# Query-state products of a retention layer as plain float32 products in 32-column strips

## The chip, the cores and the metric

The kernel runs on one core of a Trainium2 chip. The metric is the device time of one execution in microseconds. A core has five engines that run their own instruction queues: TensorE (PE, with its weight loads shown as PEld), VectorE (DVE), ScalarE (ACT), GpSimd (POOL) and SyncE (SP), which here only issues transfers.

## The reference

One inference step of a trunk of two layers, all in float32. Each layer normalizes its input, projects it to eight streams of 2048 channels, and runs a pooling branch and a retention branch that are gated, merged, projected and added to the input. There are 272 prompt tokens (16 of them learned) and 8 samples of 8 tokens each, 336 tokens in all. The part that the change touches is the retention of the samples, with a given state S of 256 x 256 for each of the 8 heads:

```python
def retention_chunk(S, q, k, v):
    ...
    scores = jnp.einsum('bihd,bjhd->bhij', q, k) * decay[None]
    intra = jnp.einsum('bhij,bjhe->bihe', scores, v)
    q_decay = jnp.exp((idx[:, None] + 1.0) * lg[None, :])
    inter = jnp.einsum('bihd,bhde->bihe', q, S) * q_decay[None, :, :, None]
    k_decay = jnp.exp((n - 1.0 - idx)[:, None] * lg[None, :])
    S_new = S * jnp.exp(n * lg)[None, :, None, None] + jnp.einsum('bjhd,bjhe->bhde', k * k_decay[None, :, :, None], v)
    return S_new, intra + inter
```

`inter` is the query-state product: 8 tokens of a sample times its own state, 8 x 256 by 256 x 256, for 8 samples, 8 heads and 2 layers.

## The kernel before

Tokens lie along the free dimension, channels along the partitions, so a projection is a product whose moving operand is the activations (128 x 336 or 128 x 320) and whose stationary operand is a block of weights. To keep float32 precision at the speed of the faster type float32r, every operand x is split into hi, x rounded to float32r (`hi_of`, line 158, on ScalarE), and lo = x - hi (`lo_of`, line 164, on VectorE), and a product is made of three: hi hi, hi lo, lo hi.

The program is one list of steps. In each step the main loop (from line 853) issues the load of a weight tile four steps ahead on SyncE's queue (`dma_step`, line 177), its split two steps ahead, then the 24 products of this step (`main_step`; every product is issued at line 154), and then the events that were put down for the step with `at`. An event's instructions go to the queues of their engines behind those of the step's products. Every head of a layer takes 16 steps (four for each of k, v, q and the gate), and its events run on into the next head's steps; `E(d, fn)` puts an event at step d of the head.

For the samples of a head it does the following. `sload(b)` loads a state (256 KB) into one of five buffers named sraw, on SyncE's queue, for samples 0 to 4 at steps 8 to 12 and for samples 5 to 7 at steps 17 to 19. `split_q` at step 12 splits q and lets GpSimd copy the sample columns of hi and lo into qpad, a tile that holds, for each half of the channels and each sample, 128 stationary columns, all zero but the sample's own 8 columns of hi and 8 of lo. `ssplit(b)` splits a state into shi and slo. `sdo(b)` at step 15 + b multiplies the 128 columns of qpad with shi and slo, both halves of the channels, into one bank of PSUM, where the products of all samples add up (each writes zeros to the rows of the others); then it makes the state's update from kts and vbd (`up`), adds it to the decayed state in place (line 423, VectorE) and stores it from GpSimd's queue (line 424). `inter_copy` at step 23 scales the bank and splits it into ithi and itlo, and `pv(2)` at step 24 adds it to the samples' outputs with two products with the matrix c01, which also sums the rows of hi and lo.

PSUM has four banks for all this (tag side). A stationary operand with few columns whose output begins at partition 0 sits in the first 32-column strip of TensorE's array; in the kernel before these are the products with 16 output rows in `pv(2)` (line 472).

`spread_rstd` (line 229) and the warm-up of 12 products before the first step are plain float32 products, and `tok` (line 313) and `back` (line 490) transpose float32 tiles.

Of the kernel before, what the change touches and what calls it, by code (L numbers as in the profile page):

```python
# [6 lines left out]
F32 = mybir.dt.float32  # L7
F32R = mybir.dt.float32r
# [6 lines left out]
NM = 16  # L15
SEQ = 256
NP = NM + SEQ
NB = 8
NS = 8
T = NP + NB * NS  # L20
HEADS = 8
HD = 256
# [15 lines left out]
C_C01 = C_GQ + 8  # L38
# [4 lines left out]
def tables():  # L43
    import numpy as np

    f = np.float32
    lg = np.log1p(-np.exp2(f(-5.0) - np.arange(HEADS, dtype=f))).astype(f).astype(np.float64)
    pos = np.concatenate([np.arange(NP), 2048 + np.tile(np.arange(NS), NB)]).astype(f)
    inv = (10000.0 ** (-np.arange(128) / 128)).astype(f)
    ang = (pos[None, :] * inv[:, None]).astype(f).astype(np.float64)  # L50
    cst = np.zeros((128, C_W), f)
    cst[:, C_ID:C_ID + 128] = np.eye(128)
    cst[:, C_COS:C_COS + T] = np.cos(ang)
    cst[:, C_SIN:C_SIN + T] = np.sin(ang)
    r = np.arange(128)
    for h in range(HEADS):
        for b in range(2):
            cst[:, C_KD + 3 * h + b] = np.exp((NP - 1 - b * 128 - r) * lg[h]) / 16
        cst[:NR2, C_KD + 3 * h + 2] = np.exp(np.where(r < NM, NM - 1 - r, NS - 1 - (r - NM) % NS) * lg[h])[:NR2] / 16
        cst[:, C_GQ + h] = np.exp((r % 8 + 1) * lg[h])  # L60
    cst[r, C_C01 + NM + r % 64] = 1
    for g, w in enumerate(WINDOWS):
        cst[:, C_RC + 16 * g:C_RC + 16 * g + 16] = 1.0 / np.minimum(w, np.arange(16) + 1)
    dt = np.zeros((HEADS, 128, SC), f)
    tok = np.arange(T)
    prompt = tok < NP
    for h in range(HEADS):
        jj, ii = tok[:, None], tok[None, :]
        same = np.where(prompt[:, None], prompt[None, :], (~prompt[None, :]) & ((jj - NP) // NS == (ii - NP) // NS))
        m = np.where(same & (ii >= jj), np.exp(np.maximum(ii - jj, 0) * lg[h]) / 16, 0)  # L70
        dt[h, :, 0:NR0] = m[0:128, 0:NP]
        dt[h, :, NR0:NR0 + NR1] = m[128:256, 128:NP]
        dt[h, :NR2, NR0 + NR1:SC] = m[256:T, 256:T]
    return {"cst": cst, "dtab": dt}, [float(np.exp(NS * x)) for x in lg]


def build(tc, a, o, g8):
    nc = tc.nc
# [6 lines left out]
    def at(s, fn, *args):  # L85
        events[s].append(lambda: fn(*args))
# [15 lines left out]
    def open_pool(name, side=None, **kw):  # L102
        P[name] = tc.alloc_tile_pool(name=name, bufs=1, side=side, reuse_waits="tile", **kw)
        return P[name]
# [15 lines left out]
    def side():  # L120
        return sidep.tile([128, 512], F32, tag="side", bufs=4, name="side")
# [4 lines left out]
    cst = cp.tile([128, C_W], F32, name="cst")  # L126
# [26 lines left out]
    def mm(out, lhsT, rhs, start, stop):  # L153
        nc.tensor.matmul(out, lhsT, rhs, start=start, stop=stop)  # L154

    def hi_of(out, in_, scale=None):
        if scale is None:
            nc.scalar.copy(out=out, in_=in_)  # L158
        else:
            nc.scalar.activation(out=out, in_=in_, func=ACTF.Copy, scale=scale)  # L160

    def lo_of(out, in_, hi, scale=None):
        if scale is None:
            nc.vector.tensor_tensor(out=out, in0=in_, in1=hi.bitcast(F32), op=ALU.subtract)  # L164
        else:
            nc.vector.scalar_tensor_tensor(out=out, in0=in_, scalar=scale, in1=hi.bitcast(F32),  # L166
                                           op0=ALU.mult, op1=ALU.subtract)
# [78 lines left out]
    H = {}  # L246

    for l in range(DEPTH):
# [12 lines left out]

        def open_r(l=l, a_side=a_side):
            p = open_pool("r", side=a_side)
            t = p.tile([128, 2, 8, 128], F32R, name="qpad")
            nc.gpsimd.memset(t.bitcast(F32), 0.0)
            H["qpad"] = t
            t = p.tile([128, SC], F32, name="sc")
            nc.gpsimd.memset(t[64:128, NR0 + NR1:SC], 0.0)
            H["sc"] = t
            t = p.tile([128, 2, 4, HD], F32R, name="vbd")  # L270
            nc.gpsimd.memset(t.bitcast(F32), 0.0)
            H["vbd"] = t
            for key in ("kt", "vt"):
                t = p.tile([128, HD], F32R, name=key + "tail")
                nc.gpsimd.memset(t[64:128].bitcast(F32), 0.0)
                H[key + "tail"] = t
# [4 lines left out]
        def head(h, l=l, c0=c0, n=n, nt=nt):  # L281
            hs = {}
            rp = lambda shape, dt, tag, bufs=1: P["r"].tile(shape, dt, tag=tag, bufs=bufs, name=tag)
# [73 lines left out]
            def split_q():  # L357
                qr = hs["qr"]
                qhi, qlo = rp([128, 2, T], F32R, "qhi"), rp([128, 2, T], F32R, "qlo")
                hi_of(qhi[:, :, n], qr[:, :, n])  # L360
                lo_of(qlo[:, :, n], qr[:, :, n], qhi[:, :, n])
                hs["q"] = qhi, qlo
                for i, s in enumerate((qhi, qlo)):
                    for d in range(2):
                        src = s[:, d, NP:T].rearrange("p (b t) -> p b t", b=8)
                        base = H["qpad"][:, d, 0, 64 * i:64 * i + 8]
                        dst = bass.AP(tensor=base.tensor, offset=base.offset, ap=[base.ap[0], [136, 8], [1, 8]])
                        nc.gpsimd.tensor_copy(out=dst, in_=src)

            def scores():  # L370
                dtab = rp([128, SC], F32, "dtab")
# [23 lines left out]
                hs["p"] = phi, plo  # L395

            def sload(b):
                s = rp([128, 2, HD], F32, "sraw", 5)
                nc.sync.dma_start(out=s, in_=a["state_ret"][l, b, h].rearrange("p (d e) -> p d e", d=2))
                hs["s", b] = s  # L400

            def ssplit(b):
                s = hs["s", b]
                hi, lo = rp([128, 2, HD], F32R, "shi", 2), rp([128, 2, HD], F32R, "slo", 2)
                hi_of(hi, s)
                lo_of(lo, s, hi)
                hs["sh", b] = hi, lo

            def sdo(b):
                if b == 0:  # L410
                    hs["inter"] = side()
                ps = hs["inter"]
                for i, x in enumerate(hs.pop(("sh", b))):
                    for d in range(2):
                        mm(ps[:, :HD], H["qpad"][:, d, b], x[:, d], b == 0 and i == 0 and d == 0,
                           b == NB - 1 and i == 1 and d == 1)
                up = side()
                for d in range(2):
                    mm(up[:, HD * d:HD * d + HD], hs["kts"][:, b // 4, 128 * d:128 * d + 128],
                       H["vbd"][:, b // 4, b % 4], True, True)  # L420
                s = hs.pop(("s", b))
                s2 = s.rearrange("p d e -> p (d e)")
                nc.vector.scalar_tensor_tensor(out=s2, in0=s2, scalar=g8[h], in1=up, op0=ALU.mult, op1=ALU.add)  # L423
                nc.gpsimd.dma_start(out=o["ret_s"][l, b, h].rearrange("p (d e) -> p d e", d=2), in_=s)  # L424
# [76 lines left out]
            E = lambda d, fn, *ar: at(b0 + d, lambda: fn(*ar))  # L501
# [10 lines left out]
            E(10 + kl, stack_out, "vt")  # L512
            E(12 + kl, stack_in, "vt")
            E(12, split_q)
            E(16, pstate)
            E(11, scores)
            E(14, scores2)
            for b in range(5):
                E(8 + b, sload, b)
            E(13, ssplit, 0)  # L520
            for b in range(NB):
                E(15 + b, sdo, b)
                if b + 1 < NB:
                    E(15 + b, ssplit, b + 1)
                if b + 5 < NB:
                    E(17 + b, sload, b + 5)
            E(17, pv, 0)
            E(18, norm2, 0)
            E(19, pv, 1)
            E(20, norm2, 1)  # L530
            E(23, inter_copy)
            E(24, pv, 2)
            E(25, norm2, 2)
            E(26, back)
# [3 lines left out]
        if l == 0:  # L538
            at(6, open_r)
        else:  # L540
            at(r0 - 1, open_r)
        for h in range(HEADS):
            head(h)
# [402 lines left out]
```

## Time and profile before

| | |
|---|---|
| median of 3 runs | 2878.2 us (2875.74 to 2878.21) |
| the profiled execution | 2874.4 us, its span 2872.7 us |
| TensorE busy | 2850.5 us (99%), 19,228 products |
| VectorE busy | 1594.3 us (55%) |
| ScalarE busy | 1001.4 us (35%) |
| GpSimd busy | 363.1 us (13%) |
| moved by DMA | 516.65 MB, 180 GB/s on average |

The rows below name an instruction by its line in the kernel, engine and operation, then the tiles (output, then inputs, where the first input named is the moving operand and the second the stationary one), the shape, and counts and times. "128*16 128x256" is a product with 128 rows and 16 columns of stationary operand and a moving operand of 256 columns. TensorE works in a pipeline, so a product lasts longer than the distance to the next one's start. "<-" behind a time of idleness names what ended it.

### The profile page before, as it was taken

What the parts mean: (1) busy time and instruction counts of PE and PEld (TensorE: products, weight loads), DVE (VectorE), ACT (ScalarE), POOL (GpSimd) and SP (SyncE); (2) the same over time, 40 slices, a digit from 0 to 9 for tenths busy, and PEclk for the clock granted to TensorE, in tenths of its full rate; (3) what the DMA queues carried; (4) which work ended last, traced back from release to release, by engine and by line L of the source; (5) the groups of instructions that cost most, each with busy time, mean ns of one, the idle gap of its engine ahead of it and who ended that gap; (6) DMA issues with size and microseconds to landing.
All of it is one profiled execution on the core that took longest, in us unless ns stands there. A gap on an engine that the chain in (4) does not pass through costs nothing.

```text
span 2872.7 us, 46777 instructions
## 1 busy us (share of the span) xinstructions
PE 2850.5 (99%) x19228; PEld 2844.3 (99%) x19228; DVE 1594.3 (55%) x2026; ACT 1001.4 (35%) x1245; POOL 363.1 (13%) x560
## 2 busy tenths in 40 slices
PE   9999999999999999999999999999999999999997
PEld 8999999999999999999999999999999999999997
DVE  7666666654345664344456666666544456644543
ACT  4333333333233333333333333333332333333332
POOL 5222222210000000000122222222100000000000
PEclk9999999999999999999999999999999999999999
DMA  6555555655454444444555665566555544444443
GB/s 225 195 200 207 204 206 203 209 199 176 160 163 155 143 151 149 143 155 166 197 179 200 209 208 208 208 207 206 204 180 180 173 145 161 144 160 162 170 161 126
DMA packets 174262, 516.65 MB, mean 180 GB/s; under 512 B 23888, under 2 KB 46672, under 8 KB 174032
## 3 DMA queue, kind: packets, MB, share of 16 engines
q1 hardware_dynamic: 150976, 447.81, 45.7%
q0 software_dynamic: 21696, 63.99, 6.2%
q8 instruction: 150, 2.46, 0.3%
q10 hardware_dynamic: 1376, 1.87, 0.2%
q14 instruction: 64, 0.52, 0.1%
HBM read 447.91 MB, written 66.57 MB: 179 GB/s over the span
## 4 chain that ended last, share of the span: by engine, by line
PE 98%; issue 1%; POOL 1%; DVE 0%; DMA 0%; ACT 0%; POOLq 0%; SPq 0%; DVEq 0%; ACTq 0%
PE acc L154 90%; PE side L154 7%; PE side L313 1%; PE side L490 0%; POOL xsq L214 0%; POOL xsq L213 0%; DMA x<-in_xT_dram 0%; DVE xf L889 0%; DVE h_lo L166 0%; DVE sinr L235 0%; POOL trs L221 0%; DVE wlo L164 0%; ACT sq L207 0%; POOLq L934 0%; DVE xs L789 0%
## 5 line engine op out<-in xcount | busy, mean ns | idle before, releaser
L154 PE MATMUL acc<-act_hi,whi 128*128 128x320 f32 (+1 forms) x3328 | 1039.7, 312 | 0.0
L154 PE MATMUL acc<-act_lo,whi 128*128 128x320 f32 (+1 forms) x3328 | 1037.5, 312 | 0.0
L154 PE MATMUL acc<-act_hi,wlo 128*128 128x320 f32 (+1 forms) x3328 | 1036.1, 311 | 0.0
L164 DVE TENSOR_TENSOR wlo<-raw,whi 128x1024 fp32r<-128x1024 f32 x720 | 870.7, 1228 | 286.5 <-ACT whi L158 277.3
L158 ACT CAST whi<-raw 128x1024 fp32r<-128x1024 f32 x720 | 738.5, 1047 | 444.7 <-PE acc L154 360.0
L154 PE MATMUL acc<-h_hi,whi 128*128 128x336 f32 x2304 | 736.6, 320 | 0.7 <-ACT whi L158 0.7
L154 PE MATMUL acc<-h_lo,whi 128*128 128x336 f32 x2304 | 733.2, 318 | 3.8 <-DVE h_lo L166 3.7
L154 PE MATMUL acc<-h_hi,wlo 128*128 128x336 f32 x2304 | 730.9, 317 | 0.7 <-DVE wlo L164 0.7
L154 PEld LDWEIGHTS acc<-act_lo,whi 128*128 128x128 f32 x3328 | 626.4, 188 | 0.0
L154 PEld LDWEIGHTS acc<-act_hi,wlo 128*128 128x128 f32 x3328 | 625.1, 188 | 0.0
L154 PEld LDWEIGHTS acc<-act_hi,whi 128*128 128x128 f32 x3328 | 624.8, 188 | 0.0
L154 PEld LDWEIGHTS acc<-h_lo,whi 128*128 128x128 f32 x2304 | 436.9, 190 | 5.3 <-DVE h_lo L166 5.2
L154 PEld LDWEIGHTS acc<-h_hi,wlo 128*128 128x128 f32 x2304 | 434.5, 189 | 1.0 <-DVE wlo L164 1.0
L154 PEld LDWEIGHTS acc<-h_hi,whi 128*128 128x128 f32 x2304 | 434.0, 188 | 0.9 <-ACT whi L158 0.9
L423 DVE SCALAR_TENSOR_TENSOR sraw<-sraw,side 128x512 f32<-128x512 f32 x128 | 87.8, 686 | 154.1 <-PE side L154 154.1
L424 POOL DMA_DIRECT2D out_ret_s_dram<-sraw x128 | 71.4, 558 | 548.2 <-DVE sraw L423 541.1
L158 ACT CAST shi<-sraw 128x512 fp32r<-128x512 f32 x128 | 79.0, 617 | 109.0 <-PE side L154 109.0
L164 DVE TENSOR_TENSOR slo<-sraw,shi 128x512 fp32r<-128x512 f32 x128 | 88.1, 688 | 0.1
L211 POOL TENSOR_TENSOR xsq<-sq 128x336 f32<-128x336 f32 (+1 forms) x3 | 3.0, 985 | 564.8 <-ACT sq L207 564.8
L160 ACT ACTIVATE kthi<-side,cst 128x256 fp32r<-128x256 f32 (+1 forms) x48 | 20.9, 468 | 137.5 <-PE side L313 137.5
L158 ACT CAST vthi<-side 128x256 fp32r<-128x256 f32 (+1 forms) x48 | 16.2, 371 | 146.3 <-PE side L313 146.3
L678 POOL DMA_DIRECT2D out_pool_u_dram<-uc x16 | 8.7, 545 | 440.5 <-DVE uc L633 440.5
(157 smaller groups left out, 2023.0 us busy)
## 6 DMA issues: line engine op xcount, KB each, us to landing
raw<-in_w_in_dram SPq DMA_DIRECT2D x512, 512.0 KB, 4.5
sraw<-in_state_ret_dram SPq DMA_DIRECT2D x128, 256.0 KB, 3.1
out_ret_s_dram<-sraw POOLq DMA_DIRECT2D x128, 256.0 KB, 3.3
raw<-in_proj_ret_dram SPq DMA_DIRECT2D x64, 512.0 KB, 4.2
raw<-in_proj_pool_dram SPq DMA_DIRECT2D x64, 512.0 KB, 5.1
raw<-in_w_out_dram SPq DMA_DIRECT2D x64, 512.0 KB, 5.2
raw<-in_pool_w_dram SPq DMA_DIRECT2D x16, 512.0 KB, 3.4
kts<-ktd SPq DMA_DIRECT2D x16, 256.0 KB, 2.9
```

Source lines behind the costliest of these rows:

```text
L154: nc.tensor.matmul(out, lhsT, rhs, start=start, stop=stop)
L158: nc.scalar.copy(out=out, in_=in_)
L160: nc.scalar.activation(out=out, in_=in_, func=ACTF.Copy, scale=scale)
L164: nc.vector.tensor_tensor(out=out, in0=in_, in1=hi.bitcast(F32), op=ALU.subtract)
L211: eng.tensor_tensor(out=xsq[:, n], in0=sq[:, 0, n], in1=sq[:, 1, n], op=ALU.add)
L313: nc.tensor.transpose(ps[:rows, 128 * d:128 * d + 128], hs[src][:, d, 128 * b:128 * b + rows], ident)
L423: nc.vector.scalar_tensor_tensor(out=s2, in0=s2, scalar=g8[h], in1=up, op0=ALU.mult, op1=ALU.add)
L424: nc.gpsimd.dma_start(out=o["ret_s"][l, b, h].rearrange("p (d e) -> p d e", d=2), in_=s)
L678: nc.gpsimd.dma_start(out=o["pool_u"][l, 2 * g + i], in_=gs.pop(("uc", i)))
```

## The change

The states are no longer split. qpad becomes a float32 tile with 32 stationary columns for each half of the channels and each sample; samples 0 to 3 use columns 0 to 7 and samples 4 to 7 columns 8 to 15, the rest stays zero. GpSimd copies the sample columns into it from q as it is before the split. A new event `inter` at step 15, ahead of the first sdo, makes all query-state products of the head: 16 plain float32 products, 2 for each sample; the outputs of samples j and j + 4 go to the rows 32 j to 32 j + 31 of the bank, which is the strip j of the array, and the loops are written so that four products in a row go to four strips. All eight states have to be on chip then, so sraw has eight buffers, and the loads stand at steps 6 to 13. `inter_copy` moves from step 23 to step 16. The matrix c01 changes with the layout of the bank. The state's update and its store stay as they were.

```diff
-    cst[r, C_C01 + NM + r % 64] = 1
+    place = r[r % 32 < 16]
+    cst[place, C_C01 + NM + 8 * (place // 32) + 32 * (place % 32 // 8) + place % 8] = 1
...
-            t = p.tile([128, 2, 8, 128], F32R, name="qpad")
-            nc.gpsimd.memset(t.bitcast(F32), 0.0)
+            t = p.tile([128, 2, 8, 32], F32, name="qpad")
+            nc.gpsimd.memset(t, 0.0)
...
-                for i, s in enumerate((qhi, qlo)):
+                for half_ in range(2):
                     for d in range(2):
-                        src = s[:, d, NP:T].rearrange("p (b t) -> p b t", b=8)
-                        base = H["qpad"][:, d, 0, 64 * i:64 * i + 8]
-                        dst = bass.AP(tensor=base.tensor, offset=base.offset, ap=[base.ap[0], [136, 8], [1, 8]])
-                        nc.gpsimd.tensor_copy(out=dst, in_=src)
+                        b0_ = NP + 32 * half_
+                        nc.gpsimd.tensor_copy(out=H["qpad"][:, d, 4 * half_:4 * half_ + 4, 8 * half_:8 * half_ + 8],
+                                              in_=qr[:, d, b0_:b0_ + 32].rearrange("p (b t) -> p b t", b=4))
...
-                s = rp([128, 2, HD], F32, "sraw", 5)
+                s = rp([128, 2, HD], F32, "sraw", 8)
...
-            def ssplit(b):
-                s = hs["s", b]
-                hi, lo = rp([128, 2, HD], F32R, "shi", 2), rp([128, 2, HD], F32R, "slo", 2)
-                hi_of(hi, s)
-                lo_of(lo, s, hi)
-                hs["sh", b] = hi, lo
+            def inter():
+                ps = hs["inter"] = side()
+                for i in range(2):
+                    for d in range(2):
+                        for j in range(4):
+                            b = 4 * i + j
+                            mm(ps[32 * j:32 * j + 32, :HD], H["qpad"][:, d, b], hs["s", b][:, d],
+                               i == 0 and d == 0, i == 1 and d == 1)
 
             def sdo(b):
-                if b == 0:
-                    hs["inter"] = side()
-                ps = hs["inter"]
-                for i, x in enumerate(hs.pop(("sh", b))):
-                    for d in range(2):
-                        mm(ps[:, :HD], H["qpad"][:, d, b], x[:, d], b == 0 and i == 0 and d == 0,
-                           b == NB - 1 and i == 1 and d == 1)
                 up = side()
...
-            for b in range(5):
-                E(8 + b, sload, b)
-            E(13, ssplit, 0)
+            for b in range(NB):
+                E(6 + b, sload, b)
+            E(15, inter)
             for b in range(NB):
                 E(15 + b, sdo, b)
-                if b + 1 < NB:
-                    E(15 + b, ssplit, b + 1)
-                if b + 5 < NB:
-                    E(17 + b, sload, b + 5)
+            E(16, inter_copy)
...
-            E(23, inter_copy)
```

## Rows read from the trace of the kernel before

**Rows 1.** The page: busy time, share and instructions; granted clock by slices; chain by engine.

```profile
PE 2850.5 (99%) x19228; PEld 2844.3 (99%) x19228; DVE 1594.3 (55%) x2026; ACT 1001.4 (35%) x1245; POOL 363.1 (13%) x560
PEclk9999999999999999999999999999999999999999
...
PE 98%; issue 1%; POOL 1%; DVE 0%; DMA 0%; ACT 0%; POOLq 0%; SPq 0%; DVEq 0%; ACTq 0%
```

**Rows 2.** Groups by shape, TensorE: count | busy us, mean ns | idle before, its ender.

```profile
L154 PE MATMUL acc<-h_hi,whi 128*128 128x336 f32 x2304 | 736.6, 320 | 0.7 <-ACT whi L158 0.7
L154 PE MATMUL acc<-h_lo,whi 128*128 128x336 f32 x2304 | 733.2, 318 | 3.8 <-DVE h_lo L166 3.7
L154 PE MATMUL acc<-h_hi,wlo 128*128 128x336 f32 x2304 | 730.9, 317 | 0.7 <-DVE wlo L164 0.7
...
L154 PE MATMUL side<-shi,qpad 128*128 128x256 f32 x256 | 51.3, 282 | 0.0
L154 PE MATMUL side<-vbd,kts 128*128 128x256 f32 x256 | 51.1, 281 | 0.0
L154 PE MATMUL side<-slo,qpad 128*128 128x256 f32 x256 | 51.0, 281 | 0.0
```

**Rows 3.** Timeline of TensorE around one sdo: start us, us, instruction.

```profile
181.56 0.31 PE L154 MATMUL acc<-h_hi,wlo 128*128 128x336 f32 x1
181.72 0.41 PE L154 MATMUL side<-shi,qpad 128*128 128x256 f32 x2
181.96 0.40 PE L154 MATMUL side<-slo,qpad 128*128 128x256 f32 x2
182.19 0.40 PE L154 MATMUL side<-vbd,kts 128*128 128x256 f32 x2
182.43 0.32 PE L154 MATMUL acc<-h_hi,whi 128*128 128x336 f32 x1
182.59 0.32 PE L154 MATMUL acc<-h_lo,whi 128*128 128x336 f32 x1
```

**Rows 4.** By tile, plain float32 products: count, ns min/median/max, first and last start, shapes.

```profile
L154 PE MATMUL side<-ones x24: 275/421/579, 1.1 to 5.7; 128*128 128x128 f32 x24
...
L154 PE MATMUL side<-cst,sinr x12: 271/275/582, 42.1 to 2859.9; 128*128 128x128 f32 x12
```

**Rows 5.** Timeline of TensorE at spread_rstd; busy time, clock by windows there.

```profile
42.62 0.35 PE L154 MATMUL side<-cst,cosr 80*128 80x80 f32 x2
42.76 0.40 PE L154 MATMUL acc<-h_hi,whi 128*128 128x336 f32 x1
...
core 0: us, PE busy (x) PEld busy (x) DVE busy (x) ACT busy (x) POOL busy (x), PEclk, DMA share, GB/s
42.00:43.00 1.00, 0.93 (x8) 0.94 (x9) 0.08 (x2) 0.00 (x1) 0.94 (x2) 1.00 0.83 322
```

**Rows 6.** Timeline and group of the float32 transposes.

```profile
186.87 0.60 PE L313 MATMUL side<-cst,tmp 128*80 128x128 f32 x4
191.02 0.38 PE L313 MATMUL side<-cst,tmp 128*128 128x128 f32 x2
...
L313 PE MATMUL side<-cst,tmp 128*128 128x128 f32 x128 | 24.4, 272 | 0.0
```

**Rows 7.** Timeline of TensorE in pv(2), where the 16-row products stand.

```profile
195.19 0.28 PE L154 MATMUL side<-vthi,plo 80*80 80x256 f32 x1
195.31 0.28 PE L154 MATMUL side<-vthi,phi 128*16 128x256 f32 x1
195.43 0.28 PE L154 MATMUL side<-vtlo,phi 128*16 128x256 f32 x1
...
195.89 0.28 PE L154 MATMUL side<-vthi,plo 128*16 128x256 f32 x1
196.00 0.28 PE L154 MATMUL side<-ithi,c 128*80 128x256 f32 x1
```

**Rows 8.** Groups by shape, weight loads.

```profile
L154 PEld LDWEIGHTS side<-shi,qpad 128*128 128x128 f32 x256 | 42.9, 188 | 0.0
...
L154 PEld LDWEIGHTS side<-vthi,plo 128*16 128x16 f32 x32 | 3.0, 94 | 0.7
```

**Rows 9.** Groups by shape, the other engines.

```profile
L164 DVE TENSOR_TENSOR slo<-sraw,shi 128x512 fp32r<-128x512 f32 x128 | 88.1, 688 | 0.1
...
L158 ACT CAST shi<-sraw 128x512 fp32r<-128x512 f32 x128 | 79.0, 617 | 109.0 <-PE side L154 109.0
...
L368 POOL CAST qpad<-qlo 128x64 fp32r<-128x64 f32 x32 | 29.2, 938 | 0.0
...
L368 POOL CAST qpad<-qhi 128x64 fp32r<-128x64 f32 x32 | 18.0, 588 | 61.8 <-ACT qhi L158 61.8
```

**Rows 10.** Waits of SyncE's queue (total us, times, longest); sraw's transfers to landing.

```profile
SPq L177 <- DVE wlo L164: 1573.7, 510, 10.3
SPq L399 <- DMA out_ret_s_dram<-sraw: 338.0, 47, 15.1
...
DMA to landing us min/median/max: 2.2/3.2/8.0
```

## The prediction

> **What bounds the kernel now.** I read the page first. TensorE is busy for 99% of the span at a granted clock of nine tenths or more in every slice, and the chain of work that ended last is 98% TensorE; VectorE is at 55% and ScalarE at 35% [rows 1]. Next come the groups of instructions by shape: before the 6,912 projection products of 336 columns TensorE idled 5.2 us in all, and before the products with the sample states, 256 of each kind, not at all [rows 2]. So in the retention stage TensorE never waits. What shortens a TensorE instruction there shortens the kernel by as much, and what is taken from any other engine gives nothing as long as that holds.
>
> A TensorE instruction must be priced by the distance from its start to the next start, not by its length: in one loop step the projection products start every 0.15 to 0.16 us although each lasts 0.32 us, since they are pipelined [rows 3]. In that step the sample work is six instructions: two products with the upper half of the state (shi), two with the lower (slo), two for the update (vbd). From the first shi to the first vbd it is 182.19 - 181.72 = 0.47 us, so a float32r product of 256 columns costs 0.118 us.
>
> **What is removed on TensorE.** Per sample the four products with shi and slo. There are 2 layers x 8 heads x 8 samples = 128 samples, which agrees with the 256 + 256 products counted [rows 2]. 128 x 0.47 = 60.2 us, all of it on the path. Per head that is 3.76 us.
>
> **What is added on TensorE.** Per head 8 samples x 2 halves = 16 plain float32 products of 256 columns. First, how many instructions is one? The kernel before has a few plain float32 products that are no transposes: spread_rstd makes two of 128 columns in each of three calls, 6 in the source, and the trace has 12 matmuls for them; the 12 warm-up products are 24 matmuls [rows 4]. So each becomes two instructions, one right behind the other, and a head gets 32. Second, what does one instruction take? Two such instructions of 80 columns take 42.76 - 42.62 = 0.14 us at a granted clock of 1.00, or 0.07 us for 80 columns, which makes 0.224 for 256 [rows 5]. The transposes, float32 too and one instruction each, give a finer figure: four of 128 columns last 0.60 us from first start to last end, the last of them 0.272, so (0.60 - 0.272) / 3 = 0.109 us for 128 columns and 0.218 for 256 [rows 6]. That is nearly twice the 0.118 of float32r. I take 0.218. The upper bound is 0.224; the lower one is 0.216, from a pair of transposes: 0.38 us less the last one's 0.272 is 0.108 [rows 6].
>
> Narrow weights do not shorten a product. The last block of each head has products with 16 output rows, and they start 0.11 to 0.12 us apart like those of 128 rows [rows 7]. So a strip of 32 columns gains only if several strips stream at once, and no row of before shows two strips at once. This is the unknown of the change, and its bounds are far apart. If nothing overlaps, a head costs 32 x 0.218 = 6.98 us. If all four strips run independently, each carries 4 products, 8 instructions, and the head costs 8 x 0.218 = 1.74 us.
>
> Between them lies what I take. The two instructions of one product go to the same strip and stand next to each other in the queue: strip 0 twice, then strip 1 twice, and so on. The trace shows matmuls starting in program order throughout, each only when the one ahead of it has streamed its columns [rows 3, 7]. If the queue keeps that order, the second instruction of strip 0 has to wait for the first, and strip 1 stands behind it. When strip 0's second starts, strip 1's first can start with it, but strip 1's second must wait again. So two instructions overlap, not four: 32 of them take 17 slots, 17 x 0.218 = 3.71 us. I choose this as it needs no reordering, which no row shows.
>
> Strips need their weights loaded too. A load of 16 columns lasts 94 ns, one of 128 columns 188 ns [rows 8], and these overlap the running products; 32 columns lie between, so I take nothing for them. The switch between full width and a strip has a row: the 16-row products already sit in the first 32-column strip, and from the last 80-row product (195.19) to the first of them (195.31), and back (195.89 to 196.00), the distance is 0.12 and 0.11 us, the same as without a switch [rows 7]. I take zero. The Trainium skill says otherwise (TensorEngine Tiling (Array Packing), Key Properties): going to another tiling mode drains the engine. Two drains per head at the 0.28 - 0.12 = 0.16 us by which a product outlasts its slot would be 16 x 2 x 0.16 = 5.1 us; the row speaks against it.
>
> **What lies off the path.** The splitting of 128 states goes: 79.0 us of ScalarE and 88.1 us of VectorE [rows 9]. TensorE waits for neither, so nothing is gained. GpSimd's 64 copies into qpad stay 64, with half the elements; at 588 and 938 ns before [rows 9] they are done three steps ahead of the new products. The memset of qpad shrinks, off the path. The copy of the products out of PSUM moves from step 23 to 16: it keeps a side bank for one step and not for eight, which takes pressure away.
>
> The eight state loads go from steps 8 to 12 and 17 to 19 to steps 6 to 13, on SyncE's queue between the weight loads, and each must find its buffer free: with eight buffers the loads of one head wait for the stores of the same samples of the head before. Behind such a wait stand the weight loads. In the trace SyncE waits 1573.7 us for buffers of the weights and 338.0 us for state stores, with no TensorE idle [rows 10]; the queue is far ahead. A state's store is issued at steps 15 to 22 of a head, its reuse stands at 22 to 29, so the new waits are shorter than the old (there a store at 15 was followed by the load at 17). I take nothing. Were the cover gone, a late state would stop TensorE for at most its landing time, 2.2 to 8.0 us [rows 10].
>
> **The sum.** Against the profiled run (2872.7 us of span, 2874.4 in all): 2874.4 - 60.2 + 16 x 3.71 = 2873.6 us, a gain of 0.8. With 0.216 or 0.224 it is 2873.0 or 2875.1. That run lies 3.8 us under the median of 2878.2 and 1.3 under the lowest of the runs, so on the median the sum says 2877.4. I give 2876, with an own range of 2870 to 2882.
>
> **Rivals.** Four strips at once: the two instructions of a strip queue in the strip and the other strips do not wait. 2874.4 - 60.2 + 16 x 1.74 = 2842.0, or 2846 on the median. For it: nothing in TensorE's work forbids it, the strips share no output. Against it: the program order of the starts. The Trainium skill (TensorE: Matmul & The Clock Gate, Part 3) measures such packs at one product's length plus about 4 ns per further tile, which would give this result; the same section calls matmuls strictly first-in first-out, which with two instructions per strip gives mine. No run here has shown either.
>
> No strips at once, the rival on the other side: float32 streams of different strips exclude each other, and 32 instructions take 6.98 us per head: 2874.4 - 60.2 + 111.7 = 2925.9, or 2930 on the median. For it: every product in the trace streams alone [rows 3, 7]. It decides as soon as fewer than 6.98 / 3.76 = 1.86 instructions overlap on average. Against it: the strips use separate columns and separate output rows.
>
> The new products wait for the eighth state: they need all eight at step 15, where the first sample needed one. Its load stands at step 13, and SyncE runs steps ahead [rows 10]. If each head lost the median landing of 3.2 us it would be 51 us more, near 2928.
>
> **How the numbers follow.** Pairs 0.42; four at once 0.36; none at once 0.17; waiting for states 0.02; something else 0.03, split between a faster and a slower end. This kernel's measurement tells 0.2%, 5.8 us, from no change. Faster is 0.36 + 0.01 = 0.37, same 0.42, slower 0.17 + 0.02 + 0.02 = 0.21. The range reaches down to four at once with the low price (2841.8, less a little) and up to the end of the pairs' own range: 2840 to 2882; what is slower by serial strips or late states stays outside with 0.2.
>
> **What would show it.** In the timeline of a head's step 15, the stretch from the first strip product to the next full-width instruction: 3.7 us by my forecast, 1.7 with four at once, 7.0 with none. The starts inside it: pairs at one moment every 0.218 us, or single starts, or four and more together. TensorE's idle before these products near zero, and the projection products at the same distance as before. ScalarE and VectorE lighter by 79 and 88 us. The prediction fails if the queue lets strips pass each other, or if float32 keeps them apart.

## The result and the profile after

| | before | after |
|---|---|---|
| median | 2877.3 us (2875.7 to 2878.2, 4 runs) | 2846.9 us (2846.2 to 2847.1, 4 runs) |
| ratio | | 0.9896, 95% interval 0.9882 to 0.9911 |
| the profiled execution, its span | 2874.4 us, 2872.7 us | 2847.1 us, 2845.3 us |

The kernel became faster by 30.5 us on the medians and by 27.4 us between the two profiled executions. That is the time of the rival "four strips at once" (2846), not that of the forecast (2876).

From the page after: busy time and share by engine, the granted clock by slices, and the chain that ended last by engine.

```profile
PE 2821.2 (99%) x19228; PEld 2796.1 (98%) x19228; DVE 1518.4 (53%) x1898; ACT 932.8 (33%) x1117; POOL 362.4 (13%) x560
PEclk9999999999999999999999999999999999999998
...
PE 98%; issue 0%; DVE 0%; POOL 0%; POOLq 0%; ACT 0%; DVEq 0%; ACTq 0%
```

TensorE bounds the kernel as in [rows 1], with the same number of matmuls, since 512 float32r ones became 512 halves of float32 products. What changed is how they lie in time. The timeline of TensorE at step 15 of a head (start us, us, instruction), against [rows 3]:

```profile
222.53 0.31 PE L155 MATMUL acc<-h_hi,wlo 128*128 128x336 f32 x1
222.77 1.93 PE L155 MATMUL side<-sraw,qpad 128*32 128x256 f32 x32
224.63 0.50 PE L155 MATMUL side<-vbd,kts 128*128 128x256 f32 x2
224.98 0.32 PE L155 MATMUL acc<-h_hi,whi 128*128 128x336 f32 x1
```

From the first strip product to the update it is 224.63 - 222.77 = 1.86 us for the whole head. How the 32 matmuls lie in it shows when the same stretch is cut into slices of one slot. Columns: slice, its length, busy time of TensorE's matmuls with the number that run in it, the same for weight loads and GpSimd, then clock and DMA.

```profile
222.76:223.00 0.24, 0.23 (x4) 0.16 (x8) 0.00 (x0) 1.00 0.00 0
223.00:223.22 0.22, 0.22 (x8) 0.13 (x4) 0.00 (x0) 1.00 0.00 0
223.22:223.43 0.21, 0.21 (x8) 0.13 (x4) 0.00 (x0) 1.00 0.00 0
...
224.30:224.51 0.21, 0.21 (x8) 0.00 (x0) 0.00 (x0) 1.00 0.85 332
```

Four start in the first slice. In each later one there are eight: the four of the slice before, which still drain, and four new ones. So four matmuls stream at once, in eight rounds: the first lasts 0.24 us, the others 0.216. That the four are of four different strips, and not two halves of two products, is settled by the kernels with fewer strips below.

### The profile page after: what moved, and what is told of

Same layout as the page of the kernel before. It is cut to its first block, busy times and chain, and to the rows that moved or that the text cites. A ratio compares the mean times of both kernels' runs of the same rounds, so it can differ in the third digit from the quotient of the medians.

```text
span 2845.3 us, 46391 instructions
## 1 busy us (share of the span) xinstructions
PE 2821.2 (99%) x19228; PEld 2796.1 (98%) x19228; DVE 1518.4 (53%) x1898; ACT 932.8 (33%) x1117; POOL 362.4 (13%) x560
## 4 chain that ended last, share of the span: by engine, by line
PE 98%; issue 0%; DVE 0%; POOL 0%; POOLq 0%; ACT 0%; DVEq 0%; ACTq 0%
PE acc L155 91%; PE side L155 6%; PE side L314 1%; PE side L485 0%; DVE xf L880 0%; DVE h_lo L167 0%; POOLq L925 0%; POOL xsq L215 0%; POOL xsq L214 0%; DVE xs L780 0%; ACT sq L208 0%; DVEq L925 0%; DVE sinr L236 0%; POOLq L214 0%; ACTq L208 0%
## 5 line engine op out<-in xcount | busy, mean ns | idle before, releaser
L582 DVE SCALAR_TENSOR_TENSOR mb<-tr,acc 128x336 f32<-128x336 f32 (+1 forms) x32 | 14.4, 493 | 81.0 <-PE acc L155 81.0
L389 DVE TENSOR_TENSOR sc<-side,dtab 128x416 f32<-128x416 f32 (+1 forms) x16 | 9.3, 583 | 90.3 <-PE side L155 90.3
```

The costliest lines, as they stand in the source:

```text
L389: nc.vector.tensor_tensor(out=sc[:, w], in0=ps[:, w], in1=dtab[:, w], op=ALU.mult)
L582: nc.vector.scalar_tensor_tensor(out=t[:, d, n], in0=H["tr", l, i][:, d, n], scalar=1.0, in1=acc[:, d, n], op0=ALU.add, op1=ALU.mult)
```

## Experiments

All experiments start from the changed kernel; its 2846.9 us and 1.86 us per head are what they are compared with. A difference per head counts 16 times. Kernels with one execution are marked so.

### Order: strip after strip

```diff
-                for i in range(2):
-                    for d in range(2):
-                        for j in range(4):
+                for j in range(4):
+                    for i in range(2):
+                        for d in range(2):
```

> The same 16 float32 strip products per head, but ordered strip by strip: the eight instructions of strip 0, then those of strip 1, and so on. Theory A (each strip has its own line; an instruction that waits for its strip doesn't hold up those of other strips behind it, as deep as needed): starts still come four by four every 0.216 us, the stretch from the first strip product to the update stays near 1.87 us per head, the time near 2847. Theory B (program order is kept, and the four at once of the changed kernel come from looking past one or two instructions only): only neighbours of different strips overlap, the stretch is 6 to 6.9 us, the time 2847 + 16 x 4.1 to 5.0 = 2913 to 2928.

Measured: 2889.9 us. In the timeline the stretch is 231.79 - 227.27 = 4.52 us:

```profile
227.27 4.59 PE L155 MATMUL side<-sraw,qpad 128*32 128x256 f32 x32
231.79 0.50 PE L155 MATMUL side<-vbd,kts 128*128 128x256 f32 x2
```

Neither A nor B as they were put. The slices of this stretch, columns as above:

```profile
227.26:227.50 0.24, 0.23 (x1) 0.14 (x2) 0.00 (x0) 1.00 0.09 34
227.50:227.72 0.22, 0.22 (x2) 0.11 (x1) 0.00 (x0) 1.00 0.05 19
227.72:227.94 0.22, 0.22 (x2) 0.11 (x1) 0.00 (x0) 1.00 0.00 0
227.94:228.16 0.21, 0.21 (x2) 0.11 (x1) 0.00 (x0) 1.00 0.00 0
228.16:228.37 0.21, 0.21 (x3) 0.14 (x3) 0.00 (x0) 1.00 0.77 152
228.37:228.58 0.21, 0.21 (x4) 0.14 (x2) 0.00 (x0) 1.00 0.98 215
```

One matmul at a time streams for four slots: strip 0 alone. Strip 1 joins in the fifth, when three of strip 0's eight matmuls are left waiting. So a waiting matmul does let those of another strip pass, but only three may wait. Counted out, 4 slots of strip 0 alone, then 4 + 4 + 4 that two strips share, and 4 of strip 3 alone make 20 slots, 20 x 0.216 = 4.32 us; the longer first slot of each strip (0.24) and the end add 0.2. The time agrees: 16 x (4.52 - 1.86) = 42.6, hence 2889.5.

### Order: the two halves of a sample in a row

```diff
                 for i in range(2):
-                    for d in range(2):
-                        for j in range(4):
+                    for j in range(4):
+                        for d in range(2):
```

> The strip products ordered by sample, both channel halves of a sample one behind the other, so that four instructions in a row go to one strip. From the strip-after-strip run: there strip 1's first product started with strip 0's fifth, that is, once three of strip 0 were left waiting. Theory A1 (every strip can hold three waiting matmuls of its own): four in a row fit, one running and three waiting, so all four strips still stream together; first strip product to the update 1.87 to 1.92 us, the time 2847 to 2848. Theory A2 (three waiting matmuls in all, over all strips): the stretch grows to about 2.5 us, the time 2847 + 16 x 0.6 = 2857.

Measured: 2848.3 us (2847.2 to 2849.2), and the stretch is 225.20 - 223.30 = 1.90 us:

```profile
223.30 1.97 PE L155 MATMUL side<-sraw,qpad 128*32 128x256 f32 x32
225.20 0.51 PE L155 MATMUL side<-vbd,kts 128*128 128x256 f32 x2
```

The first two slices of this stretch, columns as above:

```profile
223.29:223.53 0.24, 0.23 (x4) 0.18 (x8) 0.00 (x0) 1.00 0.00 0
223.53:223.75 0.22, 0.22 (x8) 0.15 (x4) 0.00 (x0) 1.00 0.00 0
```

A1 holds: with nine matmuls of other strips waiting in the queue ahead of it, strip 3's first one still starts in the first slot. The three places belong to each strip.

### Fewer strips

Two strips with four samples each (the copies into qpad and the matrix c01 follow the new layout):

```diff
...
-                for i in range(2):
+                for i in range(4):
                     for d in range(2):
-                        for j in range(4):
-                            b = 4 * i + j
+                        for j in range(2):
+                            b = 2 * i + j
...
-                               i == 0 and d == 0, i == 1 and d == 1)
+                               i == 0 and d == 0, i == 3 and d == 1)
...
-                    mm(ps[:NR2, :HD], c01, hs["it"][0], False, False)
+                    mm(ps[:NR2, :HD], c01[:64], hs["it"][0], False, False)
```

> The samples sit in two strips, four samples in each, instead of in four. Theory A (overlap of strips is what pays): each strip carries 16 instructions, 16 x 0.216 = 3.46 us per head instead of 1.73, the time 2847 + 16 x 1.73 = 2875. Rival (a 32-column float32 product is cheap in itself because its weights are narrow, or the two instructions of a product overlap): no change, 2847.

One strip, with the same loops as the changed kernel:

```diff
-                            mm(ps[32 * j:32 * j + 32, :HD], H["qpad"][:, d, b], hs["s", b][:, d],
-                               i == 0 and d == 0, i == 1 and d == 1)
+                            mm(ps[0:32, :HD], H["qpad"][:, d, b], hs["s", b][:, d],
+                               i == 0 and d == 0 and j == 0, i == 1 and d == 1 and j == 3)
...
-                    mm(ps[:NR2, :HD], c01, hs["it"][0], False, False)
+                    mm(ps[:NR2, :HD], c01[:32], hs["it"][0], False, False)
```

> All 16 products go to the first strip (the eight samples' rows are added up, so the samples' outputs are left wrong). Theory A: 32 instructions one after another, 32 x 0.216 = 6.9 us per head, the time 2847 + 16 x 5.2 = 2930. The rival that narrow weights are cheap in themselves: 2847. The gap of 0.24 us before the first strip product and of 0.31 us behind the last ones, if they belong to the change to 32 columns: still there; if they belong to the strips beside the first: gone, as at the 16-row products of before.

Measured, one execution each: 2880.0 us with two strips, 2935.8 us with one. Timelines of the two-strip kernel and then of the one-strip kernel:

```profile
226.41 0.31 PE L155 MATMUL acc<-h_hi,wlo 128*128 128x336 f32 x1
226.65 3.65 PE L155 MATMUL side<-sraw,qpad 128*32 128x256 f32 x32
230.23 0.50 PE L155 MATMUL side<-vbd,kts 128*128 128x256 f32 x2
```

```profile
233.74 0.31 PE L155 MATMUL acc<-h_hi,wlo 128*128 128x336 f32 x1
233.97 7.09 PE L155 MATMUL side<-sraw,qpad 128*32 128x256 f32 x32
241.00 0.50 PE L155 MATMUL side<-vbd,kts 128*128 128x256 f32 x2
241.34 0.32 PE L155 MATMUL acc<-h_hi,whi 128*128 128x336 f32 x1
```

The stretches are 3.58 and 7.03 us: with 4, 2 and 1 strips 1.86, 3.58, 7.03. Theory A holds; narrow weights are worth nothing in themselves, and the two matmuls of a product do not overlap, or one strip would not take 32 slots. The stretches explain 27.5 and 82.7 us, and 33.1 and 88.9 were measured. The rest, some 6 us, I had made myself without expecting it: where fewer strips are used, the product with c01 has 64 or 32 rows and not 128, and in the two-strip kernel this stands there:

```profile
343.10 0.28 PE L155 MATMUL side<-vthi,plo 128*16 128x256 f32 x1
343.31 0.34 PE L155 MATMUL side<-ithi,c 64*80 64x256 f32 x1
343.49 0.28 PE L155 MATMUL side<-itlo,c 64*80 64x256 f32 x1
343.70 0.42 PE L155 MATMUL acc<-h_hi,whi 128*128 128x336 f32 x1
343.96 0.32 PE L155 MATMUL acc<-h_lo,whi 128*128 128x336 f32 x1
```

The distances are 0.21, 0.18, 0.21 and 0.26 us, where products with 128 rows in [rows 7] keep 0.11 to 0.12 and one projection product follows another at 0.154. From the last plo product to the second projection product it is 0.86 us, 0.36 more than the 0.50 of the changed kernel (335.44 to 335.94 in its trace), and 16 x 0.36 = 5.8 us. With 32 rows, in the one-strip kernel, the same distance is 358.15 - 357.30 = 0.85 us.

### What a change to strips costs

Full width, so no strips at all:

```diff
-            t = p.tile([128, 2, 8, 32], F32, name="qpad")
+            t = p.tile([128, 2, 8, 128], F32, name="qpad")
...
-                            mm(ps[32 * j:32 * j + 32, :HD], H["qpad"][:, d, b], hs["s", b][:, d],
+                            mm(ps[:, :HD], H["qpad"][:, d, b], hs["s", b][:, d],
```

> The 16 plain float32 products with 128 stationary columns (zeros beside the sample's own), so without strips; the samples' rows are added up as in the one-strip kernel and the outputs left wrong. Both theories: 32 instructions of 0.216 us, 6.9 us per head. It tells what the gaps at the two ends belong to: if to strips, the distance from the last projection product to the first of these is 0.154 and the one behind the last 0.216, the time some 16 x 0.2 = 3 us under the one-strip kernel; if to float32, the gaps of 0.24 and 0.31 stay.

Measured, one execution: 2923.8 us. Its timeline:

```profile
231.84 0.31 PE L155 MATMUL acc<-h_hi,wlo 128*128 128x336 f32 x1
231.99 7.07 PE L155 MATMUL side<-sraw,qpad 128*128 128x256 f32 x32
238.71 0.58 PE L155 MATMUL side<-vbd,kts 128*128 128x256 f32 x2
239.13 0.32 PE L155 MATMUL acc<-h_hi,whi 128*128 128x336 f32 x1
```

The first float32 product follows at 0.15 us, as one projection product follows another; in the strip kernels at 0.24. From that last projection product to the next one, less its own slot of 0.154 and two updates of 0.118, it is 239.13 - 231.84 - 0.39 = 6.90 us, 32 x 0.216 and nothing more. In the one-strip kernel the same sum gives 241.34 - 233.74 - 0.39 = 7.21. So the change to a strip and back costs 0.31 us, and it belongs to the strip, the first one too, not to float32. The time is 12.0 us under the one-strip kernel, where some 3 had been expected: 16 x 0.31 = 5.0 us are this price, and 5.8 are the product with c01, which keeps its 128 rows here.

Two visits to the strips per head instead of one; inter(i) makes the products of four samples:

```diff
...
-            E(15, inter)
+            E(15, inter, 0)
+            E(16, inter, 1)
...
-            E(16, inter_copy)
+            E(17, inter_copy)
```

> Samples 0 to 3 at step 15, samples 4 to 7 at step 16, so the array changes to strips and back twice per head instead of once. If each change has the price read from the one-strip and full-width kernels (0.32 us for there and back, of it 0.09 before, 0.09 behind, the rest a weight load that nothing hides), the time is 2847 + 16 x 0.32 = 2852. Rival (the gaps are a wait for the states or for qpad, or a cost of the first products only): 2847.

Measured: 2853.1 us (2851.4 to 2853.6), 6.2 more than the changed kernel where 5.1 were expected. The first visit of a head in the timeline:

```profile
153.20 0.31 PE L155 MATMUL acc<-h_hi,wlo 128*128 128x336 f32 x1
153.44 1.07 PE L155 MATMUL side<-sraw,qpad 128*32 128x256 f32 x16
154.44 0.50 PE L155 MATMUL side<-vbd,kts 128*128 128x256 f32 x2
154.78 0.31 PE L155 MATMUL acc<-h_hi,whi 128*128 128x336 f32 x1
```

It is 154.78 - 153.20 - 0.39 = 1.19 us for four rounds of 0.216, so 0.33 us are the price of this visit. The price holds; the rival (a cost of the states or of the first products) falls.

The row that had spoken against the price, taken as float32:

```diff
+                        if m == 16:
+                            x, y = x.bitcast(F32), y.bitcast(F32)
                         mm(ps[:m, :HD], x[:rows, sl], y[:rows, jb], i == 0, i == tot - 1 and b < 2)
```

> The changed kernel with the six products of 16 output rows of each head (from which the prediction read that a change to a strip costs nothing) taken as plain float32 instead of float32r, on the same values. Theory 1 (float32r products with few columns use the whole array and only float32 ones go to a strip): now a gap of about 0.09 us stands before the first of them and some 0.09 us and an open weight load behind the last, as at the new strip products; 12 instructions of 0.216 instead of 6 of 0.118 and 0.28 for the change, so 16 x (1.88 + 0.28) = 35 us more, 2882. Theory 2 (the array was in a strip there all along, and the gaps at the new products have another cause, such as the states): no gaps, 16 x 1.88 = 30 us more, 2877.

Measured, one execution: 2882.9 us. The timeline, against [rows 7]:

```profile
268.82 0.28 PE L155 MATMUL side<-vthi,plo 80*80 80x256 f32 x1
269.03 0.60 PE L155 MATMUL side<-vthi,phi 128*16 128x256 f32 x2
...
271.20 0.59 PE L155 MATMUL side<-vthi,plo 128*16 128x256 f32 x2
271.73 0.34 PE L155 MATMUL side<-ithi,c 128*80 128x256 f32 x1
271.91 0.28 PE L155 MATMUL side<-itlo,c 128*80 128x256 f32 x1
```

The same products, in the same place, now have 0.21 us ahead of them, where [rows 7] have 0.12. From the last of them to the next product it is 0.53 us, 0.10 more than its two matmuls of 0.216, and the two products with c01 stand 0.18 us apart and not 0.12. Together that is about 0.25 us for the change, and 16 x (1.88 + 0.25) = 34 us of the 36.0 measured. Theory 2 falls: no state is near, and the gaps are there. Theory 1 fits, that the narrow float32r products of [rows 7] had not been in a strip. No record names the columns that an instruction uses, so this is inferred from the missing gaps.

### The splitting put back

Nothing reads the results; the first splitting stands at step 13 as before, the others one step earlier than before.

```diff
...
+            E(13, ssplit, 0)
             for b in range(NB):
+                if b + 1 < NB:
+                    E(14 + b, ssplit, b + 1)
                 E(15 + b, sdo, b)
```

> The changed kernel with the splitting of the 128 states put back (ScalarE 79 us, VectorE 88 us more, at the old steps); nothing reads the results. Theory: TensorE waits for neither engine, so the time stays at 2847, within 3 us. Rival (part of the gain came from lighter ScalarE and VectorE): between 2850 and 2860.

Measured: 2846.4 us (2845.8 to 2846.5). The groups by shape show the work, count | busy us, mean ns | idle before:

```profile
L165 DVE TENSOR_TENSOR slo<-sraw,shi 128x512 fp32r<-128x512 f32 x128 | 87.8, 686 | 3.5 <-ACT shi L159 3.4
L159 ACT CAST shi<-sraw 128x512 fp32r<-128x512 f32 x128 | 79.1, 618 | 11.7 <-DVE slo L165 11.7
```

167 us of work on two engines change nothing, so nothing of the gain came from taking them away. That TensorE's share is all of it shows in the sum further down, which closes within 0.1 us.

### The same idea on the state updates

```diff
-            def sdo(b):
-                up = side()
+            def sdo(g):
+                ups = [side() for _ in range(4)]
                 for d in range(2):
-                    mm(up[:, HD * d:HD * d + HD], hs["kts"][:, b // 4, 128 * d:128 * d + 128],
-                       H["vbd"][:, b // 4, b % 4], True, True)
+                    for j in range(4):
+                        r = slice(32 * j, 32 * j + 32)
+                        mm(ups[j][:, HD * d:HD * d + HD], hs["kts"][r, g, 128 * d:128 * d + 128],
+                           H["vbd"][r, g, j], True, True)
...
-            for b in range(NB):
-                E(15 + b, sdo, b)
...
+            E(18, sdo, 0)
...
+            E(21, sdo, 1)
```

> The changed kernel, with the same idea on the state updates: they sum over 32 rows per sample that sit at rows 32 j, so four samples take the four row strips of the array, float32r, one bank each, at steps 18 and 21 (the zero rows of vbd are left out of the product). If row strips run side by side as column strips do: per four samples 2 slots of 0.118 and a change there and back of 0.32, 0.55 us, against 8 x 0.118 = 0.94; 32 groups x 0.39 = 12 us less, 2834. Rival 1 (row strips of float32r exclude each other): 0.94 + 0.32, 32 x 0.32 = 10 us more, 2857. Rival 2 (four updates at once hold VectorE for 2.7 us and all four side banks, and TensorE waits): TensorE shows idle time in the steps behind, and the gain shrinks or turns.

Measured: 2835.7 us (2834.7 to 2837.5), 0.986 of the kernel before (0.9845 to 0.9874) and 11.2 us under the changed one. It beats both. The eight updates of four samples in its timeline:

```profile
234.64 0.31 PE L155 MATMUL acc<-h_hi,wlo 128*128 128x336 f32 x1
234.88 0.51 PE L155 MATMUL side<-vbd,kts 32*128 32x256 f32 x8
235.32 0.42 PE L155 MATMUL acc<-h_hi,whi 128*128 128x336 f32 x1
235.58 0.31 PE L155 MATMUL acc<-h_lo,whi 128*128 128x336 f32 x1
```

The eight themselves take 235.32 - 234.88 = 0.44 us, which is two rounds of 0.22 and not of the 0.118 that had been expected. From the last projection product to the second one behind the updates it is 0.94 us; less two slots of 0.154 this is 0.63, against 8 x 0.118 = 0.94 before. 32 groups x 0.31 = 10 us, of 11.2 measured. Both rivals fall: row strips of float32r run side by side, and TensorE doesn't wait, being busy for 73.00 of the 73.00 us from 183 to 256 of this trace.

## Why the prediction was right and wrong

**The frame held.** TensorE bounds the kernel, and the sum made on its start-to-start distances closes. 2874.4 - 60.2 for what is removed, and per head 224.98 - 222.53 - 0.39 = 2.06 us for what is added, gives 2874.4 - 60.2 + 16 x 2.06 = 2847.2, where the profiled run has 2847.1 (0.39 is a projection product's slot and two updates, as above). The slot was taken as 0.218 and is 0.216. That the work of ScalarE and VectorE lies off the path is shown by the splitting put back; GpSimd's, the copies into qpad, is taken up below.

**The likeliest case failed at one step:** "If the queue keeps that order, the second instruction of strip 0 has to wait for the first, and strip 1 stands behind it." In place of the 3.71 us per head that this step gave, the stretch took 1.86: four matmuls stream at once, not two. The rows that it rested on [rows 3, 7] show only products that all use the first columns of the array, so that each must wait for the one ahead. They cannot tell an order kept by the queue from one kept by the columns. With different columns a matmul that waits is passed by those of other strips, three may wait in each strip, and this order needs no more than one: the first of each strip streams, the second waits. Had the loop put a strip's eight in a row, 2.7 us of each head would have been lost. The Trainium skill (TensorE: Matmul & The Clock Gate, Part 3) gives both halves: the pack that costs little more than one product, which the slices agree with (four starts in the first 0.24 us), and matmuls that run strictly first-in first-out, which the strip-after-strip kernel contradicts (strip 1 starts in the fifth slot, with three of strip 0 still waiting).

The measured 2846.9 lies in the stated 2840 to 2882 only because that range was drawn over two cases. The forecast of 2876 with its own range of 2870 to 2882 missed by 29 us, and the likeliest outcome, no change at 0.42, did not come; four at once had been given 0.36.

**A second step was wrong and hidden by its size:** the change to strips taken at zero. Per head it is 2.06 - 8 x 0.216 = 0.33 us with the four strips' small stagger, 5 us in all: 0.09 ahead of the first strip product, 0.09 behind the last, and 0.11 us by which the second update starts late behind its weight load, the rest the stagger. The Trainium skill (TensorEngine Tiling (Array Packing), Key Properties) says that a change of tiling mode drains the engine; the gaps of 0.09 us on both sides agree with it. The 5.1 us that had been worked out by it and set aside come near the size, but by luck: two drains of 0.16 were counted, where the trace has two gaps of 0.09 and a late product. What misled was the identification, there and in the section on the kernel before: 16 output rows at partition 0 were taken for a strip, and as float32r products they show no sign of one. In the sum for four at once this term, left at zero, accounts for the distance between 2842.0 and the profiled 2847.1.

**Smaller points.** SyncE's waits for state stores of [rows 10], 338.0 us, are gone from the list of its waits after, as argued, and those for weight buffers took their place:

```profile
SPq L178 <- DVE wlo L165: 1875.2, 569, 10.3
```

The copies into qpad did not become shorter with half the elements, 840 ns on average against the 588 and 938 of [rows 9]. They are still done before the products need them, and so are the states: in the full-width kernel, with the same copies and loads, the first product follows at 0.15 us, so the gap in the changed kernel is the change's own. The rival of late states did not occur, nor did that of no strips at once (6.98 us per head).

```profile
L367 POOL COPY qpad<-tmp 128x32 f32<-128x32 f32 x64 | 52.0, 840 | 42.2 <-DVE tmp L291 41.4
```

What stays open: the medians differ by 3 us more than the two profiled runs. The profiled run of the kernel before was the fastest of all its executions (2874.4; the others 2874.7 to 2878.2).

## What to carry to other kernels

On a kernel bound by TensorE, count the zeros that its products multiply. Where the stationary side fills a quarter of the columns, or a sum a quarter of the rows, four products on four strips can stream together. Here that paid even for float32, with two matmuls per product and nearly twice the time for each: 32 of them took 1.86 us on four strips and 7.03 on one, where float32r at full width had taken 3.76. Make one visit of them, for each visit cost 0.3 to 0.4 us here. Interleave the strips in the order of issue so that no more than three wait for one strip. And before a row is taken as a witness for an array setting, make sure that its instructions use that setting.

## What the runs showed of the hardware

- A plain float32 product of 256 columns is two matmuls of 0.216 us each, with 16, 32 or 128 stationary columns; 32 such matmuls of 32 columns take 1.86 us on four column strips, 3.58 on two, 7.03 on one.
- A matmul whose strip is busy is passed by matmuls of other strips; three can wait in each strip (with eight in a row to one strip the next strip started with the fifth; four in a row held up none).
- Going to column strips and back cost 0.31 us per visit at 32 columns (one strip against full width). Float32 products with 16 columns paid about 0.25 us, float32r ones on the same values nothing.
- float32r products over 32 rows do run in row strips, eight in 0.63 us with the change. A pair of float32r products over 64 or 32 rows, one after the other between products of full height, took 0.86 and 0.85 us where 128 rows took 0.50.
